# One hybrid decoder block on one core: projection triples in pairs between attention steps, with a smaller lead over the attention

## The chip, the core and the metric

The kernel runs on one core of a Trainium2 chip. The core has a matrix engine (TensorE, PE in the profile; its weight loads are shown apart as PEld), three engines for elementwise work (VectorE = DVE, ScalarE = ACT, GpSimd = POOL) and SyncE (SP), whose queue issues all of this kernel's DMAs. The engines run side by side and wait for one another through semaphores; each works through its own instructions in the order in which the program lists them.

The metric is the device time of one execution in microseconds (us). Shown is the median of several executions.

## What is computed

One decoder layer for a sequence of 1024 tokens with 1024 channels, in float32. Cut to its core:

```python
mod = silu(c) @ w_ada + b_ada                      # six vectors of 1024
h    = rms_norm(x, g_attn_pre) * (1 + sc_a) + sh_a
proj = h @ w_in                                    # q, k, v of two mixers
oa = banded_attention(rope(qa), rope(ka), va, 127, sink=sink_a)   # 8 heads, 2 kv heads
ob = dilated_mixture_attention(rope(qb), rope(kb), vb)            # 8 heads, 3 windows
mixed = concatenate([rms_norm(oa, g_mix_a), rms_norm(ob, g_mix_b)])
x = x + gt_a * rms_norm(mixed @ w_out, g_attn_post)
h = rms_norm(x, g_mlp_pre) * (1 + sc_m) + sh_m
x = x + gt_m * rms_norm(square(relu(h @ w_up)) @ w_down, g_mlp_post)
```

## The kernel before

**A planner writes the order.** The program that is built has no free order left: a small planner in the kernel file (class `Sched`, L187 to L335) decides, while the program is built, which instruction comes next on which engine. Every piece of work is a step with a planned duration, a list of events that it depends on, and the buffers that it takes and gives back (`Res`). The planner keeps a planned clock for each engine (`sc.clk`), takes the step that can start first, writes its instructions into the program, and moves that engine's clock on. Only the order is left of this in the program; on the chip, semaphores hold the instructions to their true inputs.

**PE's streams.** For PE the steps stand in named streams, each in fixed order: `dense` (projection, output projection and MLP), `s` (attention scores), `t` (transposes of the probabilities), `pv` (probabilities times values), and small ones (`post`, `misc`, `pm`, `mod`, `fin`, `xt`, `tab`). When PE is to get its next step, `run` (L294) asks `prefer` (L2390) for an order of the streams and takes the first whose head is ready by PE's planned clock; if none is ready, it takes the one that is ready first.

**The work.** Every float32 operand of a matmul is split into a high and a low part, so a product of two tiles takes three matmuls, high by high, low by high, high by low: a *triple*. In the projection a triple is the three calls at L897, L898 and L900 for one 128-row piece of w_in against 512 tokens; eight triples make one 128-by-512 tile in PSUM (tile `pj`, two buffers), and a tile is one of three column groups c of a unit u (0 to 5) for one half x of the tokens. Units 0 and 1 hold the heads of mixer A, units 2 to 5 two heads each of mixer B. Unit 0 is done ahead by `first_unit`; the other 30 tiles, 240 triples, are the ones named in this text. After a tile's last triple `evac` rotates it, splits it, and sends q and k through DMAs at L825 to the tiles `qt` and `kt`; v is turned by PE transposes at L853 and split into `v_hl`.

**Attention steps.** An attention item (a 128-row block of mixer A, or a pair of blocks or the far half of mixer B) has steps on PE: scores `s` (L1311 for mixer A, L1156 and L1216 for mixer B), transposes `t` (L1368, L1361 and L1364, L1467) and values `pv` (L1403, L1391 to L1396, L1502). Between `s` and `t` lie a masked minimum on DVE, an exponential on ACT and a scaling mostly on POOL; between `t` and `pv` the copy of the high part on ACT and of the low part on DVE. An item is let into the `s` stream only when the projection of its unit and half is finished to the last of its three tiles (`feed_s`, with `need`).

**Lead.** `st.d` counts the projection in units (48 triples each, `tick`), `st.a` counts the attention in the same units by planned durations (`progress`; 20 us of planned PE time make one unit of mixer B). The rule of `prefer` is the core of the change:

```python
LEAD = 0.8
def prefer():
    if st.d < 5.99 and st.d - st.a < LEAD:
        return ("post", "misc", "pm", "mod", "fin", "xt", "tab", "dense", "pv", "s", "t")
    return ("post", "misc", "pm", "mod", "fin", "xt", "tab", "pv", "s", "t", "dense")
```

While the projection is less than LEAD units ahead, a projection triple goes before an attention step; otherwise attention goes first. One triple is one decision, so around the limit the two alternate.

**Beside and behind.** While this goes on, POOL works through 24 pieces of w_ada (L1045 to L1050, with sums on PE at L1063 and L1066), paced by `st.d`, and the weights of w_in are loaded and split unit by unit. When all 240 triples are done, the output projection begins (`out_block`, triples at L1799 to L1801, tile `y_ps`), in eight blocks of 128 tokens. Blocks 0 and 1 are early: they are cut into two halves, A's channels and B's channels, each with a load of the attention's output at L1721 (`f_lo` in `front`, tile `o_sb`), and their triples fill PE while the last attention items run. The other blocks have one load each. The MLP follows, PE from end to end.

## Time and profile before

| | us |
|---|---|
| median of 3 executions | 1106.89 |
| fastest and slowest of them | 1106.01, 1110.32 |
| the profiled execution's own time | 1111.09 |
| its span, first to last instruction | 1109.3 |

The profiled execution is 4.2 us over the median, and 1.8 us of its time lie outside the span. Its stages, read from what PE works on:

| stretch, us | PE works on |
|---|---|
| 0 to 68 | modulation, transposes of x, unit 0 of the projection |
| 68 to 120 | projection beside the first attention items |
| 120 to 368 | projection and attention in alternation |
| 368 to 412 | the rest of the attention, early output blocks 0 and 1 |
| 412 to 488 | output blocks 2 to 7 |
| 488 to 1109 | the MLP |

How to read it: every row of the timeline is a run of like instructions on one engine with its start, its length and, in brackets, idle time ahead of it. Matmuls are pipelined, so the length of one (about 0.39 us for 512 columns) is more than the time after which the next can start; the *pitch*, from one start to the next, is what the work takes. Idle time of an engine that is not the bottleneck costs nothing.

### The profile page before, as it was taken

To read this page: it belongs to the slowest core of one execution; us is meant where nothing else is said; L and a number is where in the kernel's file an instruction comes from. 1 tells how busy PE (TensorE), PEld (TensorE's weight loads), DVE (VectorE), ACT (ScalarE), POOL (GpSimd) and SP (SyncE) were. 2 spreads that over 40 slices of the span, in tenths; PEclk is the share of its full clock that TensorE was granted. 3 is DMA by queue.
4 is the path that set the end of the run, shared out by engine and by line. 5 is a ranking of instruction groups with operands and counts; after the bars stand their busy time and mean duration, and the time that the engine had idled before them with its cause. 6 is when DMAs were issued, how large, how long until landed. Compare 5 with 4: busy or idle time off the path is not lost.

```text
span 1109.3 us, 15373 instructions
## 1 busy us (share of the span) xinstructions
PE 1085.2 (98%) x5280; PEld 901.6 (81%) x5280; DVE 816.1 (74%) x1442; ACT 634.2 (57%) x1161; POOL 270.5 (24%) x365
## 2 busy tenths in 40 slices
PE   8999999999999999999999999999999999999996
PEld 6778888888888888788888888888888888888885
DVE  6968776667767778679797654898644996537998
ACT  7859776655456857677675244743155632347542
POOL 2447767587566641100000000000000000000002
PEclk9999999999999999999999999999999999999999
DMA  9665556453525537547731379322576043593104
GB/s 332 195 211 169 152 182 214 141 197 115 194 75 197 176 107 246 171 184 269 276 143 58 130 248 349 136 76 75 197 268 228 1 133 115 191 329 143 58 1 152
DMA packets 93631, 189.56 MB, mean 171 GB/s; under 512 B 8560, under 2 KB 33264, under 8 KB 93552
## 3 DMA queue, kind: packets, MB, share of 16 engines
q1 hardware_dynamic: 93552, 188.57, 49.3%
q8 instruction: 42, 0.69, 0.3%
q14 instruction: 37, 0.30, 0.1%
HBM read 139.25 MB, written 30.41 MB: 153 GB/s over the span
## 4 chain that ended last, share of the span: by engine, by line
PE 79%; DVE 8%; POOL 3%; issue 3%; ACT 3%; DMA 3%; SPq 1%; DVEq 0%; POOLq 0%; ACTq 0%
PE mlp_ps L2233 17%; PE mlp_ps L2234 17%; PE mlp_ps L2232 17%; PE pj L897 4%; PE pj L900 3%; PE pj L898 3%; PE y_ps L1799 2%; PE y_ps L1801 2%; PE y_ps L1800 2%; PE s_ps L1216 1%; PE o_ps L1502 1%; PE o_ps L1403 1%; PE s_ps L1311 1%; POOL ada_acc L1050 1%; PE pt_ps L1467 1%
## 5 line engine op out<-in xcount | busy, mean ns | idle before, releaser
L2232 PE MATMUL mlp_ps<-hw 128*128 128x512 f32 x896 | 349.6, 390 | 0.0
L2234 PE MATMUL mlp_ps<-hw 128*128 128x512 f32 x896 | 348.6, 389 | 0.0
L2233 PE MATMUL mlp_ps<-hw 128*128 128x512 f32 x896 | 348.6, 389 | 0.0
L2232 PEld LDWEIGHTS mlp_ps<-hw 128*128 128x128 f32 x896 | 168.2, 188 | 35.3 <-issue 0.5
L2233 PEld LDWEIGHTS mlp_ps<-hw 128*128 128x128 f32 x896 | 168.2, 188 | 35.3 <-issue 0.5
L2234 PEld LDWEIGHTS mlp_ps<-hw 128*128 128x128 f32 x896 | 168.2, 188 | 34.9
L2000 DVE TENSOR_TENSOR hw<-w,hw 128x1024 fp32r<-128x1024 f32 x94 | 112.3, 1221 | 94.0 <-ACT hw L1993 93.7
L1993 ACT CAST hw<-w 128x1024 fp32r<-128x1024 f32 x94 | 95.5, 1049 | 129.8 <-PE mlp_ps L2234 93.1
L2332 POOL TENSOR_TENSOR st<-st,nhalf 128x1 f32<-128x1 f32 x8 | 7.8, 983 | 610.2 <-DVE st L2330 610.2
L897 PE MATMUL pj<-hw,w_hl 128*128 128x512 f32 x240 | 102.7, 428 | 2.0 <-ACT vt L847 2.0
L900 PE MATMUL pj<-hw,w_hl 128*128 128x512 f32 x240 | 94.7, 395 | 0.0
L898 PE MATMUL pj<-hw,w_hl 128*128 128x512 f32 x240 | 94.5, 394 | 0.0
L1993 ACT CAST hw<-u 128x1024 fp32r<-128x1024 f32 x48 | 48.7, 1052 | 64.5 <-PE mlp_ps L2234 64.5
L2000 DVE TENSOR_TENSOR hw<-u,hw 128x1024 fp32r<-128x1024 f32 x48 | 57.1, 1220 | 18.2 <-ACT hw L1993 18.2
L2290 DVE TENSOR_TENSOR yacc<-yacc,mlp_ps 128x512 f32<-128x512 f32 x96 | 62.2, 683 | 3.3 <-PE mlp_ps L2234 3.3
L1050 POOL TENSOR_TENSOR ada_acc<-ada_acc,wa_st 128x512 f32<-128x512 f32 x42 | 55.5, 1321 | 3.5
L900 PEld LDWEIGHTS pj<-hw,w_hl 128*128 128x128 f32 x240 | 45.2, 188 | 10.4
L1799 PE MATMUL y_ps<-hw,oh 128*128 128x512 f32 x128 | 51.9, 405 | 0.4 <-ACT y_sb L1817 0.4
L897 PEld LDWEIGHTS pj<-hw,w_hl 128*128 128x128 f32 x240 | 45.4, 189 | 6.0 <-ACT vt L847 2.2
L1800 PE MATMUL y_ps<-hw,oh 128*128 128x512 f32 x128 | 49.9, 390 | 0.0
L898 PEld LDWEIGHTS pj<-hw,w_hl 128*128 128x128 f32 x240 | 45.7, 190 | 3.8 <-issue 0.2
L2271 ACT ACTIVATE u<-u 128x512 f32<-128x512 f32 x48 | 29.0, 625 | 32.9 <-DVE u L2269 32.4
(257 smaller groups left out, 1992.8 us busy)
## 6 DMA issues: line engine op xcount, KB each, us to landing
hw<-s_dram SPq DMA_DIRECT2D x84, 512.0 KB, 4.2
wa_st<-in_w_ada SPq DMA_DIRECT2D x32, 512.0 KB, 4.6
w<-in_w_up SPq DMA_DIRECT2D x32, 512.0 KB, 4.7
w<-in_w_down SPq DMA_DIRECT2D x32, 512.0 KB, 7.1
s_dram<-hw SPq DMA_DIRECT2D x28, 512.0 KB, 3.7
qt<-hl SPq DMA_DIRECT2D x40, 256.0 KB, 2.5
w_st<-in_w_in SPq DMA_DIRECT2D x36, 256.0 KB, 2.9
x_sb<-in_x SPq DMA_DIRECT2D x16, 512.0 KB, 5.7
```

The lines of the kernel that those rows point to most:

```text
L897: T.matmul(ps, w[:, 0, n], h[0], start=(k == 0), stop=False)
L898: T.matmul(ps, w[:, 1, n], h[0], start=False, stop=False)
L900: T.matmul(ps, w[:, 0, n], h[1], start=False, stop=(k == KC - 1))
L1050: G.tensor_tensor(ada.acc[:, :512], ada.acc[:, :512], wa[:, j], ALU.add)
L1799: T.matmul(ps[:], oh, wh[:, c0:c0 + 512], start=(k == 4 * m), stop=False)
L1800: T.matmul(ps[:], oh, wl[:, c0:c0 + 512], start=False, stop=False)
L1993: A.copy(out[j][0], flat(src[j]))
L2000: V.tensor_tensor(out[j][1], flat(src[j]), out[j][0].bitcast(F32), ALU.subtract)
L2232: T.matmul(ps[m][:], sh, mh, start=starts and k == 0, stop=False, **kw)
L2233: T.matmul(ps[m][:], sh, ml_, start=False, stop=False, **kw)
L2234: T.matmul(ps[m][:], sl, mh, start=False, stop=k == 3, **kw)
L2290: e = op("DVE", t_dv(512), lambda: V.tensor_tensor(y(), y(), ps[m][:], ALU.add), [e, ml.e_y[tb, n]], gives=gives, prio=1)
```

## The change

It touches the planner only; no arithmetic, no tile and no buffer changes.

1. The planner notes in `sc.runs` from which stream PE took its last step and how many of that stream it has taken in a row.
2. When a `dense` step begins such a run, the planned clock of PE is moved by a further `SWITCH`, 0.06 us. This is planned time; no instruction is added.
3. `LEAD` goes from 0.8 to 0.7.
4. With `RUN` = 2, a `dense` step is also preferred when the run of `dense` steps so far has an odd length, whatever the lead: triples come in pairs unless the next one isn't ready. The streams named ahead of `dense` still go before it.
5. In an early output block the second half's load at L1721 depends, for the planner, on the first half's load. It adds no wait that the program didn't need; it fixes the order of the two in SP's queue.

```diff
+SWITCH = 0.06
...
+        self.runs = ("", 0)
...
                 self.pe[name].pop(0)
+                self.runs = (name, self.runs[1] + 1 if self.runs[0] == name else 1)
...
+            if e == "PE" and name == "dense" and self.runs[1] == 1:
+                s += SWITCH
             self.give_out(e, o, s)
...
-            el = load(f_lo, 262144 * n, deps, takes=[] if m0 else [(r_o_, 1)], prio=-8.5 if tb == 0 else -6)
+            el = load(f_lo, 262144 * n, deps + eo.get("ld", []), takes=[] if m0 else [(r_o_, 1)],
+                      prio=-8.5 if tb == 0 else -6)
+            eo["ld"] = [el]
...
-    LEAD = 0.8
+    LEAD, RUN = 0.7, 2
 
     def prefer():
-        if st.d < 5.99 and st.d - st.a < LEAD:
+        if st.d < 5.99 and (st.d - st.a < LEAD or sc.runs[0] == "dense" and sc.runs[1] % RUN):
             return ("post", "misc", "pm", "mod", "fin", "xt", "tab", "dense", "pv", "s", "t")
```

## The prediction

> **What bounds the kernel now.** I read the page first, then the table of stretches, then PE's waits.

> ```profile
> span 1109.3 us, 15373 instructions
> PE 1085.2 (98%) x5280; PEld 901.6 (81%) x5280; DVE 816.1 (74%) x1442; ACT 634.2 (57%) x1161; POOL 270.5 (24%) x365
> ```

> PE is busy for 98% of the span; no other engine comes near. The table of stretches (columns: stretch, its length, then busy time of PE, PEld, DVE, ACT, POOL, granted clock, DMA) says where the rest lies:

> ```profile
> 68.00:120.00 52.00, 49.56 (x273) 40.92 (x271) 39.70 (x120) 39.19 (x114) 38.11 (x57) 0.97 0.69 213
> 120.00:368.00 248.00, 244.06 (x1382) 206.29 (x1381) 176.78 (x509) 154.45 (x393) 164.43 (x212) 1.00 0.49 163
> 368.00:412.00 44.00, 42.47 (x254) 36.44 (x254) 36.28 (x98) 31.13 (x73) 23.61 (x27) 1.00 0.38 116
> ```

> The change reorders PE between 68 and 412 us. There PE idles 2.44 + 3.94 + 1.53 = 7.9 us of 344. What ended that idle time, from PE's waits between 68 and 412 us (total, times, longest):

> ```profile
> PE pj L897 <- ACT vt L847: 2.0, 1, 2.0
> PE ada_ps L1066 <- POOL ada_acc L1050: 1.5, 2, 1.3
> PE x_far L1252 <- DVE z_far L1245: 0.9, 1, 0.9
> PE pm_o L1757 <- DVE o_sb L1751: 0.8, 1, 0.8
> PE o_ps L1403 <- DVE ph L1379: 0.6, 1, 0.6
> PE o_ps L1502 <- DVE ph L1483: 0.6, 1, 0.6
> ```

> These are 6.4 us in seven single events; the rest are shorter. The longest has a sequel. At 108 us attention transposes are done, the next projection triple needs a `pj` buffer, and ACT, full of exponentials, has not yet copied the old tile out. Just behind it the granted clock (the number after the busy times) falls:

> ```profile
> 111.00:115.00 4.00, 4.00 (x14) 2.70 (x13) 3.48 (x7) 1.45 (x4) 3.88 (x3) 0.57 0.61 175
> ```

> Four microseconds at 0.57 lose 4 x 0.43 = 1.7 us. So that one event is worth 2.0 + 1.7 = 3.7 us, and everything that a new order could win by never waiting is 7.9 + 1.7 = 9.6 us, 0.9% of the time.

> **The pairs.** They remove entries into projection work. In the timeline an L897 follows another stream's matmul 198 times among the 240, and an L900 42 times; the first and the last of the 198 are

> ```profile
> 71.99 0.50 PE L897 MATMUL pj<-hw,w_hl 128*128 128x512 f32 x1
> ...
> 367.82 0.45 PE L897 MATMUL pj<-hw,w_hl 128*128 128x512 f32 x1
> ```

> In pairs some 120 entries are left, so about 80 go (estimate: 198 - 240/2). What is one worth? The page seems to say something: the first matmul of a triple is slower than the second.

> ```profile
> L897 PE MATMUL pj<-hw,w_hl 128*128 128x512 f32 x240 | 102.7, 428 | 2.0 <-ACT vt L847 2.0
> ...
> L898 PE MATMUL pj<-hw,w_hl 128*128 128x512 f32 x240 | 94.5, 394 | 0.0
> ```

> 102.7 - 94.5 = 8.2 us over 198 entries are 0.041 us each, and 80 x 0.041 = 3.3 us. But a length is not a pitch. Two places of the timeline, a step of four transposes and a step of four value matmuls, each between two triples:

> ```profile
> 300.50 0.39 PE L900 MATMUL pj<-hw,w_hl 128*128 128x512 f32 x1
> 300.73 0.60 PE L1467 MATMUL pt_ps<-head,p_sb 128*128 128x128 f32 x4
> 301.08 0.47 PE L897 MATMUL pj<-hw,w_hl 128*128 128x512 f32 x1
> 301.40 0.39 PE L898 MATMUL pj<-hw,w_hl 128*128 128x512 f32 x1
> ```

> ```profile
> 308.39 0.40 PE L1391 MATMUL o_ps<-ph,v_hl 128*128 128x256 f32 x2
> 308.63 0.33 PE L1394 MATMUL o_ps<-ph,v_hl 128*128 128x128 f32 x2
> 308.80 0.44 PE L897 MATMUL pj<-hw,w_hl 128*128 128x512 f32 x1
> 309.08 0.39 PE L898 MATMUL pj<-hw,w_hl 128*128 128x512 f32 x1
> ```

> and the length of a single transpose, from the groups by line (busy, mean ns):

> ```profile
> L1467 PE MATMUL pt_ps<-head,p_sb 128*128 128x128 f32 x120 | 17.9, 273 | 0.0
> ```

> A triple's own pitch is 0.23 us (300.50 to 300.73). From the first transpose to the triple's second matmul pass 301.40 - 300.73 = 0.67 us; less 0.23 for the triple's first, 0.44 are left for four transposes, 0.11 each. Four transposes in a row are 0.60 long, one is 0.27, so their pitch among themselves is (0.60 - 0.27)/3 = 0.11 as well. L897 looks long only because it starts early, 0.03 us behind the last transpose, and then waits for its weights. The value step: 309.08 - 308.39 - 0.23 = 0.46 us for four, 0.115 each; inside, 308.39 to 308.63 gives 0.12 each for the first two. The last two leave after 0.17 together and the triple behind them loses 0.05: what the step gained at its head it pays at its end. So a narrow step costs 0.11 to 0.12 us a matmul whoever is its neighbour, and **an entry costs nothing**. I take 0 for the pairs, with 3.3 us of gain as one end of the range and, on the other side, 80 new seams between two attention steps at no more than the 0.05 that the value step shows, 4 us of loss.

> [...]

> **SWITCH** adds no instruction. It moves planned clocks by 0.06 us some 120 times, about 7 us over 300. A triple takes 0.69 us by the rows and 0.681 by the plan, so part of that is only right; I cost it at nothing, and its effect is a reshuffle of who waits, below.

> **The smaller lead.** The stretch 120 to 368 us holds 204 triples:

> ```profile
> 120.00:368.00 248.00, 86.94 (x204) 38.65 (x204) 1.00 0.49 163
> ```

> 204/48 = 4.25 units in 248 us, 58.4 us a unit, so 0.1 unit brings every attention step 5.8 us closer to the projection that feeds it. What has that much room? Of the first scores of unit 3 and of unit 5's far items the rows are, in turn: the transfers' median from issue to landing, the last k transfer ahead of each (SP's queue), and on PE the transposes of v, which end the posting, and the scores:

> ```profile
> kt<-hl SPq DMA_DIRECT2D x32, 128.0 KB, 2.1
> ```

> ```profile
> 216.12 0.60 SPq L825 DMA_DIRECT2D kt<-hl  x1
> 364.46 0.59 SPq L825 DMA_DIRECT2D kt<-hl  x1
> ```

> ```profile
> 223.26 0.60 PE L853 MATMUL pv<-head,vt 128*128 128x128 f32 x4
> 224.71 0.62 PE L1156 MATMUL s_ps<-kt,qt 128*128 128x128 f32 x4
> 370.47 0.60 PE L853 MATMUL pv<-head,vt 128*128 128x128 f32 x4
> 372.49 1.04 PE L1216 MATMUL s_ps<-kt,qt 128*128 128x256 f32 x6
> ```

> k lands at about 216.12 + 2.1 = 218.2 and 366.6; the scores start 6.5 and 5.9 us later. That is just the 5.8 us that the lead gives up. But the scores also start only 1.5 and 2.0 us behind the v transposes: an item is let in when v is posted, and posting cannot move ahead. At a unit's edge the attention will therefore run dry for a while; the planner fills the hole with triples, and the lead grows back towards 0.75 or 0.8. PE has work all the same: **0**. The end keeps its length too. The far items of unit 5 cannot start before the last tile, and the early blocks' 32 triples lie beside them; PE's other work between 120 and 368 us is 248 - 204 x 0.69 = 107 us, 25 a unit, so 2.5 us of attention move from behind the last triple to ahead of it. If the early blocks ran out as cover, these would show. The last value step and the first triple of block 2 (with `ol`):

> ```profile
> 405.54 1.17 PE L1502 MATMUL o_ps<-ph,v_far 128*128 128x128 f32 x8
> ```

> ```profile
> 412.36 0.39 PE L1801 MATMUL y_ps<-hw,ol 128*128 128x512 f32 x1
> ```

> Between 406.7 and 411.9 lie early triples alone, 5 us of cover for 2.5.

> **The ordered load.** For blocks 0 and 1 it fixes which of two transfers SP issues first:

> ```profile
> 372.19 1.49 SPq L1721 DMA_DIRECT2D o_sb<-o_dram  x3
> ```

> ```profile
> 388.24 0.36 PE L1757 MATMUL pm_o<-ones,o_sb 128*128 128x1 f32 x2
> ```

> Three of the four go out together here. Kept apart by a planned transfer, the last comes some 3 us later; what SP has queued behind it (x and w_out loads) is planned around it. The sums of the second halves on PE (L1757) came at 388.2 us and later, over 10 us of cover: 0.

> **Waits placed anew.** Every order has its own accidents. The 3.7 us event at 108 us comes before the lead binds, where attention goes first and triples fill in singly; pairs change just which triple meets the busy `pj` buffer. I give it even odds to go, -1.9, and leave the other waits as they are. The sum is 0 + 0 + 0 + 0 - 1.9, about -2 us: 1111.1 to 1109 for the profiled execution, and against the median 1106.9 to **1105**. The profiled run stood 4.2 us over the median, so I carry over the difference, not the value.

> **Rivals.**

> - *Entries cost what the planner says.* 80 x 0.06 = 4.8 us, with the 1.9 about 6.7: 1100. For it: L897's length. Against it: both sums of pitches. [...]
> - *The waits mostly go.* If two thirds of the 9.6 us vanish, -6.4: 1100.5. For it: they are single events, not a rate; against it: the new order draws its own.
> - *K arrives too late.* Mechanism: score steps stand first in line on PE at the eight edges of units 2 to 5 before k and q have landed, and PE, which cannot pass them, stops. Price: what a transfer takes over its median of 2.1 us. It decides from 0.7 us an edge (8 x 0.7 = 5.6 us); at 1.0 it is +8: 1115. For it: the room is 5.9 to 6.5 us and 5.8 go. Against it: posting of v comes later than k by more than 4 us and holds the scores back anyway.
> - *The change does little of what it says*: the lead is set by posting, pairs are broken by the streams ahead of them. Then 1107, inside the forecast.

> **How the numbers follow.** A measurement of this kernel tells about 0.5% (5.5 us) from no change; that is 1101.4 and 1112.4. Forecast, with the last rival: 62%, between 1101.4 and 1112.4, 1105 the likeliest. Entries that cost: 10%, nearly all of it faster by over 0.5%. Waits gone: 17%, faster likewise. Late k: 11%, slower. So faster 0.27, same 0.62, slower 0.11. For 8 in 10 I cut both ends: 1098 (all of the 3.3 us, the 3.7 us event and 2 us of other waits) to 1112 (4 us of seams, or five edges at 1 us).

> **What would show it.** Right: the 240 triples in some 110 to 125 runs; pitches of narrow steps still 0.11 to 0.12; PE's busy time between 68 us and the end of the attention shorter by no more than its idle time; the MLP stretch, from its first to its last matmul, unchanged. For the entries: the same count of matmuls between 68 and 488 us taking 4 us less with PE's waits unchanged. For late k: waits of L1156 or L1216 on a transfer of `kt` or `qt`. The forecast falls if the stretch up to the MLP moves by more than 5.5 us while PE's waits and the clock there do not.

## The result and the profile after

The changed kernel is slower: 1126.24 us in the median (1124.73 to 1129.21) against 1106.89 beside it, a ratio of 1.0168 (95% interval 1.0151 to 1.0186). The prediction was 1105, with a range of 1098 to 1112, and it was wrong: 19.4 us are lost where it saw about 2 won. The profiled execution took 1125.33 us, 14.2 more than that of before, so what the traces explain below is this 14.2 and not the whole 19.4: the profiled execution of before stood 4.2 us over its median, that of after 0.9 under its own.

The first two lines of the page, and the table of stretches (length, busy time of PE, PEld, DVE, ACT, POOL, granted clock, DMA), of the changed kernel:

```profile
span 1123.5 us, 15379 instructions
PE 1092.9 (97%) x5280; PEld 908.2 (81%) x5280; DVE 819.1 (73%) x1435; ACT 632.4 (56%) x1156; POOL 270.9 (24%) x376
```

```profile
68.00:120.00 52.00, 51.38 (x296) 42.91 (x294) 42.49 (x131) 41.12 (x123) 39.59 (x66) 1.00 0.59 183
120.00:368.00 248.00, 238.66 (x1319) 203.44 (x1320) 170.23 (x481) 146.74 (x369) 157.08 (x212) 0.97 0.49 158
368.00:412.00 44.00, 40.31 (x238) 33.61 (x236) 34.80 (x95) 30.28 (x74) 25.91 (x28) 1.00 0.41 136
412.00:500.10 88.10, 85.41 (x409) 69.87 (x408) 62.00 (x102) 58.96 (x92) 16.40 (x20) 0.98 0.52 179
```

The first stretch is better than before: PE idles 0.6 us in place of 2.4, and the clock is whole. The event at 108 us is gone. The loss comes after it: 248 - 238.66 = 9.3 us of idle time in place of 3.9, with a granted clock of 0.97, and 3.7 in place of 1.5 in the stretch behind. The same table, laid over the places where the clock fell:

```profile
198.60:202.00 3.40, 3.40 (x10) 2.68 (x9) 1.33 (x5) 1.60 (x5) 2.64 (x3) 0.54 0.00 0
225.90:229.30 3.40, 3.40 (x13) 2.81 (x12) 1.25 (x2) 1.65 (x3) 0.00 (x0) 0.54 0.00 0
277.10:283.90 6.80, 6.80 (x27) 6.08 (x26) 3.17 (x16) 4.01 (x13) 1.34 (x4) 0.52 0.16 50
423.90:427.30 3.40, 3.40 (x10) 2.58 (x9) 2.45 (x5) 2.30 (x4) 2.12 (x2) 0.54 0.33 112
```

These are four places with PE busy all the time at about half clock; the kernel before had one. What ended PE's idle time between 68 and 500 us (total, times, longest):

```profile
PE o_ps L1507 <- DVE ph L1488: 3.1, 1, 3.1
PE s_ps L1221 <- DVE st_far L1236: 2.7, 2, 1.6
PE pm_o L1764 <- DVE o_sb L1758: 2.5, 4, 1.7
PE o_ps L1396 <- DVE ph L1384: 1.9, 1, 1.9
PE x_far L1257 <- DVE z_far L1250: 1.2, 2, 0.8
PE pm_o L1764 <- DVE ph L1384: 1.2, 1, 1.2
PE ada_ps L1071 <- POOL ada_acc L1055: 1.1, 1, 1.1
```

(From the planner's part on, the changed file's lines lie 5 to 7 further on: L897 is L902 here, L1757 is L1764.) Single events again, as before, but other ones and more of them, and nearly all end on DVE.

To compare kernels, the time from the first of the 240 triples to the first matmul of the MLP is divided into PE's idle time, the clock's loss (for each spell its length times one minus the granted clock) and the rest, which is mainly PE's own work. In us, from the trace of one execution each:

| | before | after | difference |
|---|---|---|---|
| first triple to first MLP matmul | 417.5 | 432.2 | +14.7 |
| idle | 8.4 | 16.3 | +7.9 |
| lost to the clock | 1.7 | 8.5 | +6.8 |
| rest | 407.4 | 407.35 | 0 |
| of the 14.7, first triple to last | 299.7 | 310.5 | +10.7 |
| of the 14.7, last triple to MLP (the tail) | 117.8 | 121.8 | +4.0 |
| first to last MLP matmul | 613.3 | 613.3 | 0 |

The rest is the same, so the difference is waiting, and the clock that falls behind it. That it agrees to 0.1 us is partly luck: a matmul is 0.39 us long and the next can start after 0.23, so a short wait can hide under the length of the matmul ahead of it and be counted in the rest. Two kernels below with one order on PE, before and e_nopool_before, have rests of 407.4 and 405.0, so the split is good to 2 or 3 us.

### The profile page after: what moved, and what is told of

It reads as the page before. It is cut to its first block, busy times and chain, and to the rows that moved or that the text cites. A ratio compares the mean times of both kernels' runs of the same rounds, so it can differ in the third digit from the quotient of the medians.

```text
span 1123.5 us, 15379 instructions
## 1 busy us (share of the span) xinstructions
PE 1092.9 (97%) x5280; PEld 908.2 (81%) x5280; DVE 819.1 (73%) x1435; ACT 632.4 (56%) x1156; POOL 270.9 (24%) x376
## 4 chain that ended last, share of the span: by engine, by line
PE 65%; DVE 8%; POOL 3%; issue 2%; ACT 2%; DMA 1%; SPq 0%; DVEq 0%; POOLq 0%; ACTq 0%
PE mlp_ps L2239 17%; PE mlp_ps L2241 17%; PE mlp_ps L2240 17%; PE pj L902 2%; PE pj L905 2%; PE pj L903 2%; PE o_ps L1507 1%; PE s_ps L1221 1%; PE pt_ps L1472 1%; DVE x_sb L2341 1%; POOL p_sb L1291 1%; POOL st L1848 1%; ACT junk L1837 1%; PE y_ps L1806 1%; PE y_ps L1808 1%
## 5 line engine op out<-in xcount | busy, mean ns | idle before, releaser
L902 PE MATMUL pj<-hw,w_hl 128*128 128x512 f32 x240 | 101.7, 424 | 0.0
L1055 POOL TENSOR_TENSOR ada_acc<-ada_acc,wa_st 128x512 f32<-128x512 f32 x42 | 55.6, 1323 | 3.5
L905 PEld LDWEIGHTS pj<-hw,w_hl 128*128 128x128 f32 x240 | 46.0, 192 | 10.7
L903 PEld LDWEIGHTS pj<-hw,w_hl 128*128 128x128 f32 x240 | 46.4, 193 | 6.9 <-issue 0.2
L902 PEld LDWEIGHTS pj<-hw,w_hl 128*128 128x128 f32 x240 | 46.3, 193 | 6.9 <-issue 0.2
```

The lines of the kernel that those rows point to most:

```text
L902: T.matmul(ps, w[:, 0, n], h[0], start=(k == 0), stop=False)
L903: T.matmul(ps, w[:, 1, n], h[0], start=False, stop=False)
L905: T.matmul(ps, w[:, 0, n], h[1], start=False, stop=(k == KC - 1))
L1055: G.tensor_tensor(ada.acc[:, :512], ada.acc[:, :512], wa[:, j], ALU.add)
```

## The experiments

The table holds all of them; idle, clock loss, rest and tail are those of the table above, from one trace each, which can stand some us off its kernel's median. Every kernel but the three that say so holds the ordered load of the change, also those that are called the old order with one number changed: with the lead alone at 0.7 or 0.78, for instance, the planner would otherwise put the second half's load ahead of the first half's, which sets up the tile for both. The texts that were written ahead of the runs call these kernels "the kernel before" with one edit; they are that plus the ordered load.

| kernel | SWITCH | LEAD | RUN | other | ratio (95% interval) | idle | clock | rest | tail |
|---|---|---|---|---|---|---|---|---|---|
| before | 0 | .8 | 1 | no ordered load | 1 | 8.4 | 1.7 | 407.4 | 117.8 |
| after | .06 | .7 | 2 | | 1.0168 (1.0151 to 1.0186) | 16.3 | 8.5 | 407.4 | 121.8 |
| e_switch0 | 0 | .7 | 2 | | 1.0048 (1.0025 to 1.0071) | 13.8 | 3.4 | 405.6 | 122.7 |
| e_run1 | .06 | .7 | 1 | | 1.0091 (1.0066 to 1.0117) | 14.2 | 3.4 | 409.5 | 121.8 |
| e_lead8 | .06 | .8 | 2 | | 1.0067 (1.0044 to 1.0090) | 14.3 | 1.7 | 407.1 | 126.0 |
| e_switch_only | .06 | .8 | 1 | | 1.0108 (1.0083 to 1.0133) | 14.8 | 3.4 | 410.6 | 125.1 |
| e_run_only | 0 | .8 | 2 | | 1.0075 (1.0051 to 1.0100) | 13.8 | 5.1 | 405.2 | 123.5 |
| e_lead_only | 0 | .7 | 1 | | 1.0056 (1.0039 to 1.0073) | 13.2 | 5.1 | 405.4 | 125.2 |
| e_neg | -.02 | .8 | 1 | | 1.0073 (1.0046 to 1.0101) | 12.4 | 1.7 | 406.5 | 119.3 |
| e_all_neg | -.04 | .7 | 2 | | 1.0088 (1.0065 to 1.0111) | 11.0 | 8.5 | 405.1 | 123.6 |
| e_lead78 | 0 | .78 | 1 | | 1.0055 (1.0037 to 1.0073) | 14.3 | 0 | 406.8 | 121.2 |
| e_sure | .06 | .7 | 2 | margin .7 | 0.9990 (0.9970 to 1.0009) | 6.5 | 0 | 406.5 | 119.5 |
| e_sure03 | .06 | .7 | 2 | margin .3 | 1.0114 (1.0093 to 1.0135) | 16.3 | 6.8 | 406.2 | 126.7 |
| e_sure14 | .06 | .7 | 2 | margin 1.4 | 1.0153 (1.0128 to 1.0178) | 19.9 | 10.2 | 406.4 | 150.9 |
| e_sure_sw | .06 | .8 | 1 | margin .7 | 1.0123 (1.0098 to 1.0148) | 16.8 | 12.0 | 405.2 | 127.9 |
| e_sure_before | 0 | .8 | 1 | margin .7, no ordered load | 1.0015 (0.9994 to 1.0037) | 9.8 | 1.7 | 405.5 | 120.5 |
| e_dv | .06 | .7 | 2 | DVE planned longer | 1.0060 (1.0038 to 1.0083) | 8.1 | 0 | 405.4 | 119.1 |
| e_dv_sure | .06 | .7 | 2 | both, margin .7 | 1.0077 (1.0053 to 1.0100) | 8.7 | 1.7 | 405.8 | 124.7 |
| e_nopool | .06 | .7 | 2 | POOL without w_ada | 1.0035 (1.0020 to 1.0049) | 13.9 | 1.7 | 407.2 | 121.9 |
| e_nopool_before | 0 | .8 | 1 | the same, no ordered load | 0.9958 (0.9939 to 0.9978) | 5.6 | 0 | 405.0 | 117.6 |

**Which part carries it?** First each of the three numbers of the changed kernel alone was set back, and then the other two together, so that SWITCH alone is left (with the ordered load).

```diff
-SWITCH = 0.06
+SWITCH = 0.0              # e_switch0
-    LEAD, RUN = 0.7, 2
+    LEAD, RUN = 0.7, 1    # e_run1
+    LEAD, RUN = 0.8, 2    # e_lead8
+    LEAD, RUN = 0.8, 1    # e_switch_only
```

> The changed kernel with SWITCH = 0 (pairs and LEAD 0.7 kept). Theory C, the plan is too slow on PE: with 0.06 us a run the plan gives PE 1.42 us for a pair that takes 1.39 on the chip, so PE comes to its attention steps earlier than their inputs were planned for; then most of the 19 us go, ratio to before 1.000 to 1.006, idle time of PE between the first L902 and the first MLP matmul back from 16 to about 9 us. Theory P, pairs themselves: two attention steps back to back leave too little time for DVE; then nothing goes, ratio 1.013 to 1.020. Theory L, the lead: the same as P here.

> The changed kernel with RUN = 1: single triples, LEAD 0.7, SWITCH 0.06. Theory P: back to before, ratio 0.998 to 1.005. Theory L: 1.013 to 1.020. Theory C: with some 200 runs instead of 116 the plan of PE is out by more (0.05 us for each single triple), so as slow as the change or slower, 1.015 to 1.025.

> The changed kernel with LEAD = 0.8: pairs and SWITCH 0.06 kept. Theory L: back to before, ratio 0.998 to 1.005. Theories P and C: 1.013 to 1.020.

> The kernel before with SWITCH = 0.06 alone: single triples, LEAD 0.8. Theory C: slower, ratio 1.01 to 1.02, with PE idle 15 us or more ahead of the MLP. Theories P and L: same as before, 0.997 to 1.004.

Each part taken out wins back 0.8 to 1.2%: 1.0048, 1.0091 and 1.0067. But SWITCH alone, with the old lead and single triples, costs 1.1%. Were it one part, taking out the other two would have left the loss as it was, and taking out that one would have removed it all. No part did either. Next came the two remaining corners, and SWITCH below zero.

```diff
-SWITCH = 0.06
+SWITCH = 0.0              # e_run_only, e_lead_only
+SWITCH = -0.02            # e_neg
+SWITCH = -0.04            # e_all_neg, with LEAD, RUN = 0.7, 2
-    LEAD, RUN = 0.7, 2
+    LEAD, RUN = 0.8, 2    # e_run_only
+    LEAD, RUN = 0.7, 1    # e_lead_only
+    LEAD, RUN = 0.8, 1    # e_neg
```

> The kernel before with SWITCH = -0.02 alone: the plan gives PE 0.02 us less for each run of triples, so planned PE runs further ahead of the chip's. Theory C (the plan's PE must not be slower than the chip's): 0.994 to 1.002, idle of PE ahead of the MLP 9 us or less. Theory N (the order of before happens to meet few accidents, and any other order, whatever the reason for it, meets the usual number): 1.004 to 1.011, idle 13 to 16 us.

> The changed kernel with SWITCH = -0.04 in place of +0.06 (pairs, LEAD 0.7). Theory C: under e_switch0's 1.0048, 0.995 to 1.003. Theory N: 1.004 to 1.011, no better than e_switch0. If pairs or lead cost something themselves (P or L): 1.004 to 1.011 too.

> The kernel before with pairs alone (RUN 2, LEAD 0.8, SWITCH 0). Theory C: 0.998 to 1.003. Theory P: 1.005 and more, as e_switch0. Theory N: 1.004 to 1.011.

> The kernel before with LEAD 0.7 alone (single triples, SWITCH 0). Theory C: 0.998 to 1.003. Theory L: 1.005 and more, with waits of the first score steps of a unit. Theory N: 1.004 to 1.011.

With these, the eight corners of the three numbers are complete. The corners with SWITCH at 0.06 have a mean ratio of 1.0109, those without it 1.0045; the smaller lead makes 1.0091 against 1.0063, pairs 1.0090 against 1.0064. One of the eight is the kernel before itself, and it alone makes the last two differences: without it they are 1.0091 against 1.0083, and 1.0090 against 1.0085. Only SWITCH keeps one, 1.0109 against 1.0060. From the kernel before, every single step (with the ordered load) costs 0.6 to 1.1%, and from the changed kernel every single step back wins 0.8 to 1.2%. The parts don't add up (the three single steps sum to 2.4%, the whole is 1.7%). That the planned clock of PE is too slow and SWITCH therefore bad falls with the two negative values: they speed the plan up, and cost 0.7 and 0.9% too.

**Does the smallest new order cost as much?** The four kernels of the next group set LEAD to 0.78 and nothing else; give every PE stream other than `dense` a margin, so that its step counts as ready only 0.7 us after the plan says so (in the changed kernel and in the kernel before); and plan 0.084 us more for each DVE instruction priced by `t_dv` or `t_d2`.

```diff
-SURE = dict(s=0.0, t=0.0, pv=0.0, post=0.0, fin=1.0)
+SURE = dict(s=0.7, t=0.7, pv=0.7, post=0.7, fin=1.0, misc=0.7, pm=0.7)   # e_sure, e_sure_before
...
-    LEAD = 0.8
+    LEAD, RUN = 0.78, 1                                                 # e_lead78
...
 def t_dv(n):
-    return 0.066 + 0.00104 * n
+    return 0.15 + 0.00104 * n                                           # e_dv, t_d2 likewise
```

> The changed kernel, whose planner lets PE take an attention step (s, t, pv, post, misc, pm) ahead of its turn only when its inputs have been ready for 0.7 us by the plan (SURE 0.7 instead of 0). Theory M (PE waits because the plan places steps with no margin, and what comes late is up to 1 us late): idle of PE ahead of the MLP from 16 to under 10 us, clock loss under 3.5 us, ratio 0.998 to 1.007. Theory N (any new order meets 12 to 16 us): no less idle, ratio 1.004 to 1.017.

> The changed kernel with DVE's planned durations longer by 0.084 us an instruction, as the trace shows them (0.69 us for 512 elements, planned 0.60). Theory D (waits come because the plan has DVE done too early): idle from 16 to under 10 us, ratio 0.998 to 1.007. Theory N, and a theory in which DVE is late for reasons that no duration holds (POOL holding it up): idle 12 to 16 us, ratio 1.004 to 1.017.

> The kernel before with the same margin of 0.7 us. Theory M: idle under 8.4 us, ratio 0.992 to 1.001. Theory N: a new order like any other, idle 12 to 16 us, ratio 1.004 to 1.011.

> The kernel before with LEAD 0.78 alone, an edit too small to matter by itself: one triple is 0.021 unit. Theory N: still 1.004 to 1.011, with idle plus clock loss of 14 to 20 us where before has 10. If instead the size of an edit decides: 0.998 to 1.003.

A lead of 0.78 in place of 0.8 costs 0.55%, as much as 0.7 does (0.56%). So the size of the step does not set the price. That a new order as such pays it is the reading from here on; the ordered load, which both kernels hold, could be part of it. The kernel before with the margin and without the ordered load stood at 1.0015, less than the 1.004 that theory N expected at least. Longer DVE times gave 1.0060 with 8.1 us of idle time, as theory D expected, from a trace that is among the fastest of that kernel's runs. The margin brought the changed kernel level with the kernel before (0.9990, the interval includes 1), with 6.5 us of idle time and a whole clock. That looked like a cure. A cure must depend on its dose and help another order too:

```diff
+SURE = dict(s=0.3, t=0.3, pv=0.3, post=0.3, fin=1.0, misc=0.3, pm=0.3)   # e_sure03
+SURE = dict(s=1.4, t=1.4, pv=1.4, post=1.4, fin=1.0, misc=1.4, pm=1.4)   # e_sure14
+SURE = dict(s=0.7, t=0.7, pv=0.7, post=0.7, fin=1.0, misc=0.7, pm=0.7)   # e_sure_sw, e_dv_sure
```

(e_sure_sw has the lead and the single triples of e_switch_only, e_dv_sure the longer DVE times of e_dv.)

> The changed kernel with a margin of 0.3 us. Theory M: between the change and e_sure, 1.002 to 1.012, idle ahead of the MLP 7 to 14 us. Theory N: a draw like the others, 1.004 to 1.017.

> The changed kernel with a margin of 1.4 us. Theory M: idle no more than e_sure's 6.5 us by much, under 10, no clock loss to speak of, 0.994 to 1.004; if attention then comes too late for its tail, up to 1.008 with waits at the end of the attention. Theory N: 1.004 to 1.017, idle 11 to 16 us.

> The changed kernel with both DVE's durations of the trace and the margin of 0.7 us. Theory M: 0.993 to 1.002, idle under 8 us. Theory N: 1.004 to 1.017.

> Single triples, LEAD 0.8, SWITCH 0.06 (the kernel of e_switch_only) with the margin of 0.7 us. Theory M: from 1.0108 to 0.997 to 1.004, idle from 14.8 to under 10 us. Theory N: 1.004 to 1.011, idle 12 to 16 us.

It is none. A margin of 0.3 leaves 1.0114, with 16.3 us of idle time where theory M expected 7 to 14, and 1.4 leaves 1.0153, though there the tail of 150.9 us shows that it also moves work behind the last triple; with 0.7 the order of e_switch_only goes from 1.0108 to 1.0123, and the better DVE times make the good result worse, 1.0077. So the 0.9990 reads as one more draw. Over the 17 new orders so far, the change among them, the ratio lies between 0.9990 and 1.0168 with a mean of 1.0080, and idle time and clock loss together are 17.5 us in the mean, against 10.1 before and 24.9 after.

**What is a wait made of?** Two of the longest waits after were then followed back. PE's value step stops for 3.1 us at 221.8 us. Its row, the DVE instructions ahead of it, and POOL's (start, length, instruction) in the changed kernel:

```profile
224.92 0.73 PE L1507 MATMUL o_ps<-ph,v_hl 128*128 128x128 f32 x3 [3.08 <-DVE ph L1488]
```

```profile
219.40 0.58 DVE L1281 TENSOR_TENSOR st_far<-st_far,d_far 128x16 f32<-128x16 f32 x1
...
220.46 0.91 DVE L1284 TENSOR_TENSOR a_far<-a_far,d_far 128x8 f32<-128x8 f32 x1
221.40 2.87 DVE L1291 TENSOR_SCALAR p_sb<-p_sb,a_far 128x256 f32<-128x256 f32 x3
224.20 0.67 DVE L1488 TENSOR_TENSOR ph<-pt_ps,ph 128x512 fp32r<-128x512 f32 x1
```

```profile
219.27 0.69 POOL L1054 TENSOR_SCALAR wa_st<-wa_st,cond 128x512 f32<-128x512 f32 x1 [1.02 <-DMA wa_st<-in_w_ada]
220.04 1.30 POOL L1055 TENSOR_TENSOR ada_acc<-ada_acc,wa_st 128x512 f32<-128x512 f32 x1
221.33 0.69 POOL L1054 TENSOR_SCALAR wa_st<-wa_st,cond 128x512 f32<-128x512 f32 x1
222.10 1.26 POOL L1055 TENSOR_TENSOR ada_acc<-ada_acc,wa_st 128x512 f32<-128x512 f32 x1
```

DVE's L1281 has 16 elements a row and ends at 219.98, with POOL's L1054 (219.96); L1284 has 8 and ends at 221.37, with L1055 (221.34); the first of the L1291 lie over the next two. The second wait is of the same kind: at 273.3 us an L1281 of 16 elements takes 1.24 us, beside a POOL L1055 of 1.67, and 1.9 us of waiting on PE follow. So POOL's w_ada work was left out of both kernels, every other engine's order kept; the six vectors of the modulation then lack POOL's pieces.

```diff
                 else:
-                    G.tensor_scalar(wa[:, j], wa[:, j], cj, 1.0, ALU.mult, ALU.mult)
-                    G.tensor_tensor(ada.acc[:, :512], ada.acc[:, :512], wa[:, j], ALU.add)
+                    pass
+                    pass
```

> The changed kernel with every other engine's order untouched, but POOL's share of the w_ada work left out: its multiply (L1054) and its add (L1055) by the piece of w_ada are gone, so the six vectors of the modulation are summed from a part of the pieces only (some 42 pairs of instructions fewer). Theory K (most of the new waits come from VectorE being held up by POOL's w_ada instructions, as in the 3.1 us wait at 221 us and the 1.9 us wait at 273 us): between the first projection matmul and the first MLP matmul the idle time of PE falls from 16 to under 10 us and the loss to the clock from 8.5 to under 3.5; ratio to the kernel before at most 1.006. Rival theory O (the waits come from the new order of VectorE's and ScalarE's own queues; POOL only happens to be busy at the two places): idle time stays at 13 us or more, ratio 1.010 or more.

> The kernel before with the same part of POOL's w_ada work left out (L1049 and L1050), all orders untouched: what the removal is worth where few waits end on VectorE. Theory K: idle time between the first projection matmul and the first MLP matmul falls from 8.4 to 5 to 7 us, of it the 1.5 us of PE's waits for the w_ada sums; ratio 0.996 to 0.999, so the gap between the two kernels shrinks from 0.0168 to under 0.008. Rival theory O: the ratio is the same, 0.996 to 0.999, and the gap between the two kernels stays at 0.012 or more.

The same DVE instructions, now with POOL idle between 218.1 and 220.25 us, in e_nopool:

```profile
219.25 0.17 DVE L1281 TENSOR_TENSOR st_far<-st_far,d_far 128x16 f32<-128x16 f32 x1
...
219.89 0.17 DVE L1284 TENSOR_TENSOR a_far<-a_far,d_far 128x8 f32<-128x8 f32 x1
220.09 1.06 DVE L1291 TENSOR_SCALAR p_sb<-p_sb,a_far 128x256 f32<-128x256 f32 x2
```

0.17 us each in place of 0.58 and 0.91, and L1291 0.53 apiece in place of 0.96. In the changed kernel the two ended at 219.98 and 221.37, 0.02 and 0.03 us behind a POOL instruction each, which reads as if DVE had been held until POOL was done; by what, the runs don't show. (For L1291 they show the two times only.) PE's waits in e_nopool, between 68 and 500 us:

```profile
PE s_ps L1221 <- DVE st_far L1236: 2.9, 3, 1.6
PE pm_o L1764 <- DVE o_sb L1758: 2.7, 4, 1.9
PE s_ps L1316 <- DMA qt<-hl: 2.5, 1, 2.5
PE px L1875 <- ACT xn L1864: 1.9, 3, 0.8
PE pm_o L1764 <- DVE ph L1384: 1.4, 1, 1.4
PE o_ps L1507 <- DVE ph L1488: 0.6, 1, 0.6
```

The 3.1 and 1.9 us on `ph` and the 1.1 us on `ada_acc` are gone (the last by leaving out what it waited for), and with them the clock's falls at 199, 226 and 277 us. The gap between the two orders goes from 1.0168 to 1.0035/0.9958 = 1.0077 (some 0.0024 either way, the two half intervals taken together). So 0.0091 of 0.0168, about half (10 of 19 us, give or take 3), came from the changed order's meeting with POOL's w_ada work. The two gaps were measured in different rounds, in which the kernel before stood at 1106.89 and at 1109.16. Not all was as theory K expected: idle time is 13.9 us and not under 10. Of it 2.5 us are the wait on `qt` from 75.5 us on, which the trace of the changed kernel, with the same order, doesn't have, and whose clock loss of 1.7 comes on top; this execution stands 3.7 us over its kernel's median. Without it 11.4 are left.

Those are mostly in the tail, and there both orders are unmoved by POOL: 117.8 and 117.6 us for the old, 121.8 and 121.9 for the new. The last column of the table says more: all 17 new orders have a longer tail than before, 119.1 us the shortest. The waits differ from one to the next. With LEAD at 0.7 alone (e_lead_only), and with 0.78 alone (e_lead78), the two longest of the tail are

```profile
PE y_ps L1806 <- ACT oh L1747: 4.0, 1, 4.0
PE y_ps L1806 <- DVE y_sb L1830: 2.1, 1, 2.1
```

```profile
PE s_ps L1221 <- DVE st_far L1236: 2.7, 1, 2.7
PE y_ps L1806 <- DVE y_sb L1830: 1.4, 1, 1.4
```

One late wait is common, though. The kernel before issues the load of output block 2 (`o_sb`) ahead of the last four stores of the attention's output. In all eleven new orders without a margin, e_dv among them, two of these stores go first. The rows of before, then those of after on SP, ACT and PE:

```profile
390.67 0.38 SPq L1721 DMA_DIRECT2D o_sb<-o_dram  x1
401.96 8.36 SPq L1533 DMA_DIRECT2D o_dram<-ot  x4
```

```profile
411.03 1.09 SPq L1538 DMA_DIRECT2D o_dram<-ot  x2
412.22 0.54 SPq L1726 DMA_DIRECT2D o_sb<-o_dram  x1
416.55 1.05 ACT L1747 CAST oh<-o_sb 128x1024 fp32r<-128x1024 f32 x1 [2.53 <-DMA o_sb<-o_dram]
423.03 0.58 PE L1764 MATMUL pm_o<-ones,o_sb 128*128 128x1 f32 x4 [1.72 <-DVE o_sb L1758]
```

ACT waits 2.5 us for the block, what DVE and ACT do with it comes late, and PE stops 1.7 us for its sum; the clock's fall at 424 us follows. In each of the eleven a wait of 1.1 to 2.1 us on PE comes within 7 us of the block's arrival, and in the three that were followed back (after, e_lead78, e_lead_only) it goes back to this load: on the sum, or on a `y_sb` step that stands behind block 2's in DVE's queue. The kernel before has no wait over 0.4 us there, and the six orders with a margin keep the load ahead of the stores. So this part of the tail is not drawn afresh; nearly every new order shares it.

**What stays open.** Why every other order has the longer tail isn't settled as a whole; the six with a margin have it without the late load. The ordered load stands in all but one of them (e_sure_before, tail 120.5) and was not run by itself. With the three numbers at their old values it would change SP's queue alone: an output store changes places with a load, one load of the four `o_sb` comes later, the load of block 2 keeps its place ahead of the stores, and the other engines' orders stay as they were. What that alone costs is not known, so a part of the 0.8% that new orders cost in the mean may be its own. Nor is it settled whether SWITCH as such costs: its ten orders with 0.06 have a mean of 1.0095 and the seven others 1.0059, about two standard errors apart. POOL's w_ada work was taken out of two orders only.

## Why the prediction was wrong

The first matmul of a triple after, in the groups by line (busy, mean ns):

```profile
L902 PE MATMUL pj<-hw,w_hl 128*128 128x512 f32 x240 | 101.7, 424 | 0.0
```

- **The pairs: right.** 116 runs of triples in place of 199 (110 to 125 were expected), a length of 424 ns where L897 had 428, and a rest of 407.35 us against 407.4. Over all the kernels tried the rest has a mean of 406.2 us with pairs and 406.9 without, and single values from 405.0 to 410.6. An entry costs nothing that can be told from this scatter: the means differ by 0.7 us, where 80 entries at the planner's 0.06 us would have made 4.8.
- **The smaller lead: right in what it looked at.** By the planner's own counters the lead stayed near 0.7 (0.66 to 0.82) over the triples that ran from 120 to 368 us, PE had work, and no score step waited on `kt` or `qt` in the changed kernel; the rival of late K did not come. "The end keeps its length too" was wrong: the tail grew by 4.0 us. Its cover was counted as triples only. In the tail 2.5 us of waits fall on the sums of `o_sb`, 1.7 of them behind the late load of block 2, which the prediction did not look at.
- **The ordered load: not contradicted**, and not shown by itself.
- **SWITCH: the wrong turn begins here.** "A reshuffle of who waits" is what it is, but it was costed at nothing. As the only number changed, with the ordered load, it cost 1.08%.
- **Waits placed anew: the step that failed.** It took the old order's 9.6 us of idle time and clock loss for the usual amount, gave even odds that 3.7 of them go, and left "the other waits as they are". The event at 108 us did go, and the clock's fall behind it. But the other waits don't stay: after, idle time and clock loss were 24.9 us. The runs read as if most of what a new order meets is drawn afresh, from orders whose usual sum is 17.5 us; about half of this loss is shown to come from POOL's w_ada work, and why new orders are worse in general stays open. The rival on the slow side was a mechanism with a place, K at eight edges; it should have been this redraw, with 7 us as the usual price (17.5 - 10.1). The old order stands at the low end of what this planner gives (of the seventeen only e_sure and e_dv wait and lose less), and from there a redraw mostly goes up; no row of the profile before said so.
- **And idle time was priced once.** The prediction saw that 2.0 us of waiting at 108 us cost 3.7, but added single events at face value elsewhere. After, 7.9 us more of idle time brought 6.8 us more of clock loss. That is more than usual: over the 17 new orders the means are 13.2 us of idle time and 4.3 of clock loss.
- Its own test, "the forecast falls if the stretch up to the MLP moves by more than 5.5 us while PE's waits and the clock there do not", did not trip: the stretch moved by 14.7 us, and waits and clock moved by just that. The mechanism was the one of the forecast, its size and sign were not.

## What to carry to other kernels

Where a planner fixes the order ahead of time, a change of one of its numbers is not a local edit: every order meets its own waits, and the first question is where the present order stands among the others, which a few runs with harmless nudges (here 0.78 for 0.80) tell before any gain is computed. Judge a rule of such a planner by the mean over several nudged orders, not by one, for a good result like 0.9990 didn't survive a change of dose. And look in the trace for waits whose cause the planner can't know, such as tiny DVE instructions beside POOL's additions (0.91 us in place of 0.17 here): those are worth planning for, since POOL's w_ada work stood behind about half of this loss.
